# Four weight buffers at the start of the u stage, expert rows of v gathered from the end of the u stage with a pause, and the second gate tile loaded earlier

## The chip, the cores and the metric

The kernel runs on one core of one Trainium2 chip as a single launch. The metric is device time in microseconds (us), the median of several runs. Before the change it is 2059.68 us, the median of 3 runs that lie between 2057.51 and 2063.43. The profiled execution, from which every duration below is taken, took 2052.94 us, and its instructions span 2051.2 us.

## The reference, cut to what matters

The reference is a decoder trunk of two layers on 256 tokens of width 1024. Each layer adds three things to x: a mixer (stick-breaking attention beside chunkwise retention), cross-attention to 256 memory rows, and an expert network with product-key retrieval. A final RMSNorm ends it. The change touches the expert network alone:

```python
def peer_ffn(h, w_pq, sub_keys, expert_u, expert_v):     # shortened
    q = (h @ w_pq).reshape(B, S, PEER_HEADS, 2, PEER_DQ // 2)
    scores = jnp.einsum('bshpd,hpkd->bshpk', q, sub_keys)
    top_s, top_i = lax.top_k(scores, K)                  # 16 of 128 keys, twice per head
    ...                                                  # 16 best of the 256 sums: expert_idx, gate
    u = jnp.take(expert_u, ic, axis=0)
    a = jnp.einsum('cd,chkd->chk', hc, u)
    w = gc * jax.nn.gelu(a, approximate=False)
    return jnp.einsum('chk,chkd->cd', w, jnp.take(expert_v, ic, axis=0))
```

There are 16384 experts of one neuron each, and a token uses 8 heads x 16 of them. `peer_u` and `peer_v` are 64 MB per layer each.

## The kernel before, in words

For 224 of the 256 tokens the kernel does not gather experts. It multiplies the whole of `peer_u` with the tokens (the **u stage**), applies the GELU to all 16384 x 224 products, multiplies them by gates that are zero for every expert a token did not choose, and multiplies the result with the whole of `peer_v` (the **v stage**). For the last 32 tokens it gathers rows of `peer_u` and `peer_v` (4 per step and token, on 128 partitions), 32 steps each.

**The weight stream.** All weights pass through the class `Stream`. A *pair* is 1 MB (128 partitions x 2048 floats) and serves two *units* of 128 x 1024. A layer has 42 pairs ahead of the experts, then 64 pairs for u and 64 for v, so the u stage has units 0 to 127, and so has the v stage. `load` issues the pair loads on SP's queue, into one of two own buffers `raw`, or into a buffer of the list `more` while the pair's number is not over `last`. `prep` splits a unit for the fp32r matmuls: ScalarE copies it to `hi` (L74), VectorE subtracts to get `lo` (L76). It stands two units ahead of the matmuls; there are three `hi` and `lo` tiles. After the second half of a pair is split its buffer is free, and `load` issues the next pair into it; SP's queue waits for that subtraction. A unit of u is 24 matmuls of 224 columns (L1150, L1151, L1153), a unit of v 16 (8 of 448 columns, 8 of 224; L1213, L1215).

**Side work.** The code is a fixed order on each engine. After each unit `side.tick()` advances every side task by one step (`yield`), so a side task's instructions stand between those of the units:

- `peer_task` selects the experts, scatters the gates of tokens 128 to 223 into the DRAM table `gd` by indirect adds on GpSimd (L920), and builds the gates of tokens 0 to 127 in the SBUF tile `gt` (16 x 1024 floats per partition, `g_build`).
- `gather_u` gathers rows of u (L1028 on GpSimd) into two buffers `rows` and reduces them on VectorE (L1069) to the weights `wg`. It ends when all 32 are reduced and all scatters are issued.
- `gather_v` gathers 32 times rows of v (L1028) into the same two buffers, and VectorE adds each, weighted, to `hacc` (L1091, L1093). Before the change it is started when the v stage starts, and does one gather every 3, 3 and 4 units. At its end it adds the sums to x in four additions (L1102 to L1110).

**The activated values.** In the u stage `ev_u` writes the GELU of tokens 128 to 223 into `act`, a tile of 128 x 128 x 96 floats, two of the 128 slices after every second unit, in order. The other 128 tokens go to DRAM (`tdr`), or straight into `gt` once that is complete.

**The gate tiles.** `w_load(n)` loads for pair n of v the gates from `gd` (L1174) and the activated values from `tdr` (L1179); its tiles are `tt_` for even n and `oh` for odd n, two buffers of each name. `w_mul` multiplies them on GpSimd and VectorE (L1185, L1187), `w_hi` and `w_lo` split the product (ScalarE L1202, VectorE L1207). The v matmuls of units 2n and 2n+1 wait for `w_lo(n)`. `w_load(0)` waits for the last scatters.

In the v stage two parts of `gt` that have been used join the list `more` after units 18 and 34, so that from there the stream has three and then four buffers; in the u stage it has two.

Of the kernel before, what the change touches and what calls it, by code (L numbers as in the profile page):

```python
# [132 lines left out]
def build(tc, ctx, a):  # L133
# [27 lines left out]
    st = Stream(tc, ctx, units)  # L161
    side = Side()
# [34 lines left out]
    def unit(f):  # L197
        hi, lo = st.get()
        f(hi, lo)
        flush()  # L200
        side.tick()
# [55 lines left out]
    def b_units(src, n, evac, first=0):  # L257

        for i in range(first, first + n):
            if i % 2 == 0:  # L260
                ps = mm.tile([128, 2, 256], F32, name="mm")

            def f(hi, lo):
                h3 = hi.rearrange("p (k n) -> p k n", k=KT)
                l3 = lo.rearrange("p (k n) -> p k n", k=KT)
                o = ps[:, i % 2]
                for k in range(KT):
                    T.matmul(o, h3[:, k], src[:, k, 0:256], start=(k == 0), stop=False)  # L268
                    T.matmul(o, h3[:, k], src[:, k, 256:512], start=False, stop=False)  # L269
                for k in range(KT):  # L270
                    T.matmul(o, l3[:, k], src[:, k, 0:256], start=False, stop=(k == KT - 1))  # L271
            unit(f)
            if i % 2:
                pend.append(lambda i=i, ps=ps: evac(i // 2, ps))
# [92 lines left out]
    for l in range(L):  # L367
# [654 lines left out]
        def rows_():  # L1022
            return gp.tile([128, D], F32, name="rows", bufs=2)

        def gather(rows, j):

            r = rows_()
            G.indirect_dma_start(r, None, rows, bass.IndirectOffsetOnAxis(ap=eg[:, 0, j:j + 1], axis=0))  # L1028
            return r
        go = []  # L1030

        def gather_u():

            hr = gp.tile([128, D], F32, name="hacc")
            gn = rows_()
            row = a["peer_norm"][l]
            nc.scalar.dma_start(gn, bass.AP(tensor=row.tensor, offset=row.offset, ap=[[0, 128], [1, D]]))
            V.tensor_scalar(hr[T0:128], x[T0:128, 1], rx[T0:128, 1:2], None, op0=OP.mult)
            yield
            yield  # L1040
            for q in range(3):
                nc.sync.dma_start(hr[TG * q:TG * q + TG], hr[T0:128])
            yield
            yield
            V.tensor_mul(hr, hr, gn)
            pool_us, since, n, done, ready = 0.0, 0, 0, 0, 0
            rs = deque()
            while done < 32 or held:
                if go and not ready:
                    ready = 1  # L1050
                    for q in range(4):
                        nc.sync.dma_start(eg[TG * q:TG * q + TG], ge[T0:128, :, 32 * q:32 * q + 32])
                pool_us = min(pool_us + POOL[0], 2 * POOL[0])
                while pool_us > 0:
                    if ready > 2 and n < 32 and len(rs) < 2 and (since >= 2 or not held):
                        rs.append((gather(u_rows, n), ready))
                        n, since = n + 1, 0
                        pool_us -= POOL[2]
                    elif held:
                        if next(held[0], held) is held:  # L1060
                            held.popleft()
                            continue
                        since += 1
                        pool_us -= POOL[1]
                    else:
                        break
                if rs and rs[0][1] + 3 < ready:
                    r, _ = rs.popleft()
                    V.tensor_tensor_reduce(r, r, hr, 1.0, 0.0, op0=OP.mult, op1=OP.add,  # L1069
                                           accum_out=wg[:, done:done + 1])  # L1070
                    credit[0] -= 1.25
                    done += 1
                ready += ready > 0
                yield
            A.activation(wg, wg, AF.Gelu)
            yield
            V.tensor_mul(wg, wg, eg.bitcast(F32)[:, 1])

        def gather_v():

            for _ in range(2):
                yield
            acc = gp.tile([128, D], F32, name="hacc")
            rs = deque()
            for j in range(33):
                if j < 32:
                    rs.append(gather(v_rows, j))
                if j >= 1:
                    r = rs.popleft()
                    if j == 1:  # L1090
                        V.tensor_scalar(acc, r, wg[:, 0:1], None, op0=OP.mult)  # L1091
                    else:
                        V.scalar_tensor_tensor(acc, r, wg[:, j - 1:j], acc, op0=OP.mult, op1=OP.add)  # L1093
                for _ in range(3 + (j % 3 == 2)):
                    yield
            parts = []
            for q in range(3):
                r = rows_()
                nc.sync.dma_start(r[T0:128], acc[TG * q:TG * q + TG])
                parts.append(r)  # L1100
                if q == 1:
                    V.tensor_add(x[T0:128, 1], x[T0:128, 1], acc[T0:128])  # L1102
                    yield
                    yield
                    yield
                    V.tensor_add(x[T0:128, 1], x[T0:128, 1], parts.pop(0)[T0:128])
            for r in parts:
                yield
                yield
                V.tensor_add(x[T0:128, 1], x[T0:128, 1], r[T0:128])  # L1110
# [15 lines left out]
        credit = [0.0]  # L1126
        t_p = side.add(paced(peer_task(), credit, RATE))
        t_g = side.add(gather_u())
        b_units(hTp, 14, ev_q, 2)
        flush()  # L1130
        side.drain(t_h)
# [2 lines left out]
        act = pool(c_g0, "act", side="right").tile([128, 128, T0], F32, name="act")  # L1134
# [3 lines left out]
        def u_units(first, n):  # L1138

            for i in range(first, first + n):  # L1140
                if i % 2 == 0:
                    u_ps[0] = mm.tile([128, 2, 256], F32, name="mm")
                ps = u_ps[0]

                def f(hi, lo):
                    h3 = hi.rearrange("p (k n) -> p k n", k=KT)
                    l3 = lo.rearrange("p (k n) -> p k n", k=KT)
                    o = ps[:, i % 2, 0:TD]
                    for k in range(KT):
                        T.matmul(o, h3[:, k], hT[:, k, 0:TD], start=(k == 0), stop=False)  # L1150
                        T.matmul(o, h3[:, k], hT[:, k, 256:256 + TD], start=False, stop=False)  # L1151
                    for k in range(KT):
                        T.matmul(o, l3[:, k], hT[:, k, 0:TD], start=False, stop=(k == KT - 1))  # L1153
                unit(f)
                if i % 2:
                    pend.append(lambda i=i, ps=ps: ev_u(i // 2, ps))
# [53 lines left out]
        def v_mm(i, w, hi, lo, ds=(4, 5, 6, 7, 0, 1, 2, 3)):  # L1210

            for d in ds:
                T.matmul(out[d][:, 0:2 * TD], hi[:, d * 128:d * 128 + 128], w[:, i % 2].rearrange("p a t -> p (a t)"),  # L1213
                         start=(i == 0), stop=False, skip_group_check=True)
                T.matmul(out[d][:, 0:TD], lo[:, d * 128:d * 128 + 128], w[:, i % 2, 0],  # L1215
                         start=False, stop=(i == 127), skip_group_check=True)
        u_units(0, 124)
        flush()
        assert not t_p in side.tasks and not t_g in side.tasks
        w_load(0)  # L1220
        u_units(124, 2)
        w_mul(0)
        w_hi(0)
# [1 line left out]
        w_lo(0)  # L1225
        u_units(127, 1)
        flush()
        w_load(1)
        w_load(2)
        c_ps.close()  # L1230
        ops = pool(c_ps, "ops", space=PS)
        out = [mm.tile([128, 512], F32, name="mm") for d in range(4)]
        out += [ops.tile([128, 512], F32, name=f"out{d}") for d in range(4, 8)]
        t_v = side.add(gather_v())
        st.last = (st.n + 126) // 2
        for i in range(126):
            n = i // 2
            if i % 2 == 0:
                for m in {0: (), 1: (3, 4), 2: (5, 6)}.get(n, (n + 4,)):
                    w_load(m)  # L1240
                if n in (9, 17):
                    st.more.append(gt[0][:, 2 * n - 18:2 * n - 2].rearrange("p c t -> p (c t)"))
                w_mul(n + 1)
                w = ww.pop(n)
            else:
                w_lo(n + 1)

            def f(hi, lo):
                v_mm(i, w, hi, lo)
                if i % 2 == 0:  # L1250
                    w_hi(n + 1)
            unit(f)
# [151 lines left out]
```

## Time and profile before

| | before |
|---|---|
| median of 3 runs | 2059.68 us (2057.51 to 2063.43) |
| the profiled execution's own time | 2052.94 us |
| span of its instructions | 2051.2 us |
| TensorE busy (matmuls) | 2000.3 us, 98% of the span |
| VectorE / ScalarE / GpSimd busy | 1590.0 / 1109.5 / 787.5 us |
| mean granted TensorE clock | 0.994 of full speed |
| DMA | 499.63 MB, 244 GB/s on average |
| u stages, first to last unit | 304 to 692 us and 1317 to 1707 us |
| v stages, first to last unit | 692 to 1020 us and 1707 to 2038 us |

The u stage starts with the first matmul of L1150 and the v stage with the first of L1213. TensorE's busy time is the union of its matmuls; a gap in it is time in which it waited. "Idle before" and "<-" name what ended such a wait.

### The profile page before, as it was taken

To read this page: it belongs to the slowest core of one execution; us is meant where nothing else is said; L and a number is where in the kernel's file an instruction comes from. 1 tells how busy PE (TensorE), PEld (TensorE's weight loads), DVE (VectorE), ACT (ScalarE), POOL (GpSimd) and SP (SyncE) were. 2 spreads that over 40 slices of the span, in tenths; PEclk is the share of its full clock that TensorE was granted. 3 is DMA by queue.
4 is the path that set the end of the run, shared out by engine and by line. 5 is a ranking of instruction groups with operands and counts; after the bars stand their busy time and mean duration, and the time that the engine had idled before them with its cause. 6 is when DMAs were issued, how large, how long until landed. Compare 5 with 4: busy or idle time off the path is not lost.

```text
span 2051.2 us, 37324 instructions
## 1 busy us (share of the span) xinstructions
PE 2000.3 (98%) x14564; PEld 1906.1 (93%) x14564; DVE 1590.0 (78%) x2691; ACT 1109.5 (54%) x1573; POOL 787.5 (38%) x569
## 2 busy tenths in 40 slices
PE   8999999999999999999999999999999998999997
PEld 7899899999999989999988998999999998999997
DVE  5775598988877578888876756899888765888887
ACT  5645555544566545555566445654456664455554
POOL 0120028778765123332112100477767632232321
PEclk9999999999999999999999999999999999999999
DMA  7655457899876689999566545578988766999983
GB/s 251 222 208 179 149 178 197 244 284 285 266 230 199 239 312 340 322 318 314 171 229 249 182 165 178 162 211 262 281 263 281 228 182 231 327 339 323 320 298 127
DMA packets 189250, 499.63 MB, mean 244 GB/s; under 512 B 77329, under 2 KB 124561, under 8 KB 144401
## 3 DMA queue, kind: packets, MB, share of 16 engines
q1 hardware_dynamic: 138800, 421.12, 59.5%
q0 software_dynamic: 47104, 67.23, 13.0%
q10 hardware_dynamic: 3168, 8.90, 1.3%
q8 instruction: 113, 1.85, 0.4%
q14 instruction: 65, 0.52, 0.1%
HBM read 478.40 MB, written 33.91 MB: 250 GB/s over the span
## 4 chain that ended last, share of the span: by engine, by line
PE 70%; DVE 12%; DMA 10%; issue 5%; ACT 3%; SPq 0%; POOL 0%; ACTq 0%; POOLq 0%; DVEq 0%
PE mm L1213 8%; PE out L1213 8%; DVE lo L76 6%; PE mm L1151 5%; PE mm L1150 5%; PE mm L1153 5%; DMA raw<-u 5%; PE mm L1215 4%; PE out L1215 4%; PE mm L211 4%; PE mm L213 4%; PE mm L212 4%; PE mm L269 3%; PE mm L271 3%; PE mm L268 3%
## 5 line engine op out<-in xcount | busy, mean ns | idle before, releaser
L74 ACT CAST hi<-raw 128x1024 fp32r<-128x1024 f32 x580 | 607.6, 1052 | 573.0 <-DMA raw<-u 196.1
L76 DVE TENSOR_TENSOR lo<-raw,hi 128x1024 fp32r<-128x1024 f32 x580 | 714.1, 1238 | 259.8 <-ACT hi L74 252.8
L920 POOL DMA_INDIRECT gd<-gv,gi x256 | 438.8, 1714 | 187.6 <-issue 82.8
L1150 PE MATMUL mm<-hT,hi 128*128 128x224 f32 x2048 | 480.9, 279 | 8.9 <-ACT hi L74 8.5
L1151 PE MATMUL mm<-hT,hi 128*128 128x224 f32 x2048 | 474.2, 276 | 0.0
L1150 PEld LDWEIGHTS mm<-hT,hi 128*128 128x128 f32 x2048 | 396.8, 194 | 11.4 <-ACT hi L74 10.3
L1151 PEld LDWEIGHTS mm<-hT,hi 128*128 128x128 f32 x2048 | 396.2, 193 | 0.0
L1213 PE MATMUL out<-hT,hi 128*128 128x448 f32 x1008 | 333.5, 376 | 12.7 <-DVE hT L1207 12.7
L1213 PE MATMUL mm<-hT,hi 128*128 128x448 f32 x1008 | 331.1, 374 | 0.0
L1153 PE MATMUL mm<-hT,lo 128*128 128x224 f32 x2048 | 274.2, 277 | 3.5 <-DVE lo L76 3.5
L1215 PE MATMUL out<-hT,lo 128*128 128x224 f32 x1008 | 266.8, 265 | 0.0
L1215 PE MATMUL mm<-hT,lo 128*128 128x224 f32 x1008 | 266.4, 264 | 0.0
L1153 PEld LDWEIGHTS mm<-hT,lo 128*128 128x128 f32 x2048 | 251.4, 193 | 5.5 <-DVE lo L76 4.8
L1213 PEld LDWEIGHTS out<-hT,hi 128*128 128x128 f32 x1008 | 189.6, 188 | 30.5 <-DVE hT L1207 16.2
L1213 PEld LDWEIGHTS mm<-hT,hi 128*128 128x128 f32 x1008 | 189.3, 188 | 14.4
L1215 PEld LDWEIGHTS out<-hT,lo 128*128 128x128 f32 x1008 | 192.8, 191 | 0.0
L1215 PEld LDWEIGHTS mm<-hT,lo 128*128 128x128 f32 x1008 | 192.5, 191 | 0.0
L1028 POOL DMA_INDIRECT rows<-v_rows,eg x64 | 87.0, 1359 | 217.9 <-DVE hacc L1093 205.6
L74 ACT CAST hi<-gt 128x1024 fp32r<-128x1024 f32 x100 | 104.9, 1049 | 116.0 <-PE mm L1213 93.3
L76 DVE TENSOR_TENSOR lo<-gt,hi 128x1024 fp32r<-128x1024 f32 x100 | 126.0, 1260 | 37.4 <-ACT hi L74 37.1
L277 POOL TENSOR_TENSOR rstd<-rstd,mhalf 128x2 f32<-128x2 f32 (+1 forms) x8 | 5.5, 688 | 302.7 <-DVE rstd L317 302.7
L1028 POOL DMA_INDIRECT rows<-u_rows,eg x64 | 97.9, 1530 | 57.4 <-DVE wg L1069 39.8
(710 smaller groups left out, 3274.9 us busy)
## 6 DMA issues: line engine op xcount, KB each, us to landing
raw<-u SPq DMA_DIRECT2D x128, 1024.0 KB
raw<-v SPq DMA_DIRECT2D x78, 1024.0 KB
gt<-v SPq DMA_DIRECT2D x50, 1024.0 KB
raw<-w_in_a SPq DMA_DIRECT2D x20, 1024.0 KB
gd<-zeros SPq DMA_DIRECT2D x64, 256.0 KB
raw<-pq SPq DMA_DIRECT2D x16, 1024.0 KB
raw<-wkv_b SPq DMA_DIRECT2D x8, 1024.0 KB
raw<-w_out SPq DMA_DIRECT2D x8, 1024.0 KB
```

What stands on the lines that cost most here:

```text
L74: self.nc.scalar.copy(hi, r)
L76: self.nc.vector.tensor_sub(lo, r, hi.bitcast(F32))
L211: T.matmul(ps[tt], sh, h3[:, kk], start=(k == 0), stop=False)
L212: T.matmul(ps[tt], sl, h3[:, kk], start=False, stop=False)
L213: T.matmul(ps[tt], sh, l3[:, kk], start=False, stop=(k == KT - 1))
L920: i_ = G.indirect_dma_start(gd[l], bass.IndirectOffsetOnAxis(ap=gi[0:T0, h, c:c + 1], axis=0), gv[0:T0, h, c:c + 1], None, compute_op=OP.a ...
L1028: G.indirect_dma_start(r, None, rows, bass.IndirectOffsetOnAxis(ap=eg[:, 0, j:j + 1], axis=0))
L1150: T.matmul(o, h3[:, k], hT[:, k, 0:TD], start=(k == 0), stop=False)
L1151: T.matmul(o, h3[:, k], hT[:, k, 256:256 + TD], start=False, stop=False)
L1153: T.matmul(o, l3[:, k], hT[:, k, 0:TD], start=False, stop=(k == KT - 1))
L1213: T.matmul(out[d][:, 0:2 * TD], hi[:, d * 128:d * 128 + 128], w[:, i % 2].rearrange("p a t -> p (a t)"), start=(i == 0), stop=False, skip_ ...
L1215: T.matmul(out[d][:, 0:TD], lo[:, d * 128:d * 128 + 128], w[:, i % 2, 0], start=False, stop=(i == 127), skip_group_check=True)
```

## The change

Three edits. First, when the u stage starts, the last third of `act` (two parts of 2048 floats per partition, slices 85 and up) joins the list `more`, and `last` allows it for the first 40 of the 64 pairs, units 0 to 79. `act` slice 84 and up are written after unit 85. The list is cleared when the v stage starts. Second, `gather_v` is added as a side task together with `gather_u` and begins when `gather_u` has ended. Its spacing follows the number of units since the start of the u stage: 2 units before unit 122, then until unit 146 (unit 18 of v) a pause, then (246 - unit) / (rounds left). Third, `w_load(1)` stands right behind `w_load(0)`, four units earlier than before.

```diff
-        go = []
+        go, u0 = [], []
 ...
         def gather_v():
 
-            for _ in range(2):
+            while t_g in side.tasks:
                 yield
 ...
-                for _ in range(3 + (j % 3 == 2)):
+                at = st.n - u0[0]
+                for _ in range(2 if at < 122 else 146 - at if at < 146 else max((246 - at) // (33 - j), 1)):
                     yield
 ...
         t_g = side.add(gather_u())
+        t_v = side.add(gather_v())
 ...
+        u0.append(st.n)
+        st.last = (st.n + 78) // 2
+        for i in (4, 5):
+            st.more.append(act.rearrange("p i t -> p (i t)")[:, 2048 * i:2048 * i + 2048])
         u_units(0, 124)
         flush()
         assert not t_p in side.tasks and not t_g in side.tasks
         w_load(0)
+        w_load(1)
         u_units(124, 2)
 ...
         flush()
-        w_load(1)
         w_load(2)
 ...
-        t_v = side.add(gather_v())
         st.last = (st.n + 126) // 2
+        st.more.clear()
```

The line numbers behind the second edit grow by 1 or 2: L1163 (the store to `tdr`) is L1165 after, L1174 and L1179 are L1176 and L1181, L1185 is L1187.

SP's queue at the start of the first u stage. `raw0` and `raw1` are the stream's own buffers, `act` is the tile of activated values, `tdr` stores are those of `ev_u`. Before:

```order
L62 DMA raw0_71<-u 128x2048
L62 DMA raw1_72<-u 128x2048
L62 DMA raw0_71<-u 128x2048
L62 DMA raw1_72<-u 128x2048
L1163 DMA tdr_99<-tt__3155 128x256
L62 DMA raw0_71<-u 128x2048
L1163 DMA tdr_99<-tt__3248 128x256
```

Now:

```order
L62 DMA raw0_71<-u 128x2048
L62 DMA raw1_72<-u 128x2048
L62 DMA raw0_71<-u 128x2048
L62 DMA act_3045<-u 128x2048 x2
L62 DMA raw1_72<-u 128x2048
L1165 DMA tdr_99<-tt__3157 128x256
L62 DMA raw0_71<-u 128x2048
L1165 DMA tdr_99<-tt__3250 128x256
L62 DMA act_3045<-u 128x2048
```

Two more pairs are issued ahead of the first store, so that each later load stands four pairs ahead of its use and not two.

SP's queue where the u stage ends; `tt_` and `oh` are gate tiles, `gd0` is the gate table. Before:

```order
L1163 DMA tdr_99<-tt__8048 128x256
L62 DMA raw0_71<-v 128x2048
L1174 DMA tt__8084<-gd0_97 128x2x96
L1179 DMA tt__8084<-tdr_99 128x2x128
L62 DMA raw1_72<-v 128x2048
L62 DMA raw0_71<-v 128x2048
L1174 DMA oh_8216<-gd0_97 128x2x96
L1179 DMA oh_8216<-tdr_99 128x2x128
L1174 DMA tt__8219<-gd0_97 128x2x96
```

Now:

```order
L1165 DMA tdr_99<-tt__8054 128x256
L62 DMA raw1_72<-v 128x2048
L1176 DMA tt__8090<-gd0_97 128x2x96
L1181 DMA tt__8090<-tdr_99 128x2x128
L1176 DMA oh_8093<-gd0_97 128x2x96
L1181 DMA oh_8093<-tdr_99 128x2x128
L62 DMA raw0_71<-v 128x2048
L62 DMA raw1_72<-v 128x2048
L1176 DMA tt__8225<-gd0_97 128x2x96
```

The second gate tile (`oh_8216` before, `oh_8093` now) moved ahead of two pair loads of v.

GpSimd at the same place; `rows<-v_rows` are the gathers, the L1185 (now L1187) rows are `w_mul`. Before:

```order
L920 DMA gd0_97<-gv_4027,gi_4028 2097152x1 x14
L1185 TENSOR_TENSOR tt__8084<-tt__8084,act_3045 128x2x96
L1185 TENSOR_TENSOR oh_8216<-oh_8216,act_3045 128x2x96
L1185 TENSOR_TENSOR tt__8219<-tt__8219,act_3045 128x2x96
L1028 DMA rows_8310<-v_rows,eg_2351 128x1024
L1185 TENSOR_TENSOR oh_8280<-oh_8280,act_3045 128x2x96
L1028 DMA rows_8385<-v_rows,eg_2351 128x1024
L1185 TENSOR_TENSOR tt__8283<-tt__8283,act_3045 128x2x96
L1185 TENSOR_TENSOR oh_8334<-oh_8334,act_3045 128x2x96
L1028 DMA rows_8462<-v_rows,eg_2351 128x1024
```

Now:

```order
L920 DMA gd0_97<-gv_4029,gi_4030 2097152x1 x14
L1028 DMA rows_7936<-v_rows,eg_2351 128x1024
L1028 DMA rows_8020<-v_rows,eg_2351 128x1024
L1187 TENSOR_TENSOR tt__8090<-tt__8090,act_3045 128x2x96
L1187 TENSOR_TENSOR oh_8093<-oh_8093,act_3045 128x2x96
L1187 TENSOR_TENSOR tt__8225<-tt__8225,act_3045 128x2x96
L1187 TENSOR_TENSOR oh_8286<-oh_8286,act_3045 128x2x96
L1187 TENSOR_TENSOR tt__8289<-tt__8289,act_3045 128x2x96
L1187 TENSOR_TENSOR oh_8337<-oh_8337,act_3045 128x2x96
```

Two gathers stand ahead of the first gate product; the third follows the tenth product (`oh_8484`), where before five gathers stand in between.

## Rows read from the trace of the kernel before

**Rows 1.** The page: span, TensorE, and who TensorE waited for (waits view).

```profile
span 2051.2 us, 37324 instructions
...
PE 2000.3 (98%) x14564; PEld 1906.1 (93%) x14564; DVE 1590.0 (78%) x2691; ACT 1109.5 (54%) x1573; POOL 787.5 (38%) x569
...
PE out L1213 <- DVE hT L1207: 12.7, 12, 3.0
PE mm L1150 <- ACT hi L74: 8.5, 6, 2.6
...
PE mm L1153 <- DVE lo L76: 3.5, 7, 0.9
...
PE sps L986 <- DVE gs L981: 1.7, 2, 1.3
```

**Rows 2.** Windows: stretch, length, busy us of five engines (instructions), clock, DMA share, GB/s.

```profile
300.00:400.00 100.00, 99.86 (x892) 99.68 (x891) 92.82 (x299) 59.18 (x92) 79.37 (x46) 1.00 0.76 214
400.00:550.00 150.00, 143.26 (x1236) 140.73 (x1236) 129.93 (x272) 74.11 (x114) 115.37 (x71) 0.99 0.91 280
675.00:775.00 100.00, 94.11 (x634) 88.90 (x633) 70.43 (x79) 47.33 (x62) 24.28 (x28) 1.00 0.82 287
775.00:800.00 25.00, 25.00 (x162) 23.86 (x160) 21.69 (x24) 12.98 (x16) 7.96 (x8) 1.00 0.98 357
825.00:975.00 150.00, 150.00 (x960) 143.18 (x959) 128.31 (x139) 78.11 (x90) 48.09 (x47) 1.00 0.93 317
1300.00:1400.00 100.00, 99.87 (x886) 99.68 (x885) 92.77 (x289) 60.88 (x96) 72.31 (x42) 1.00 0.70 199
1400.00:1575.00 175.00, 167.87 (x1438) 165.87 (x1437) 150.37 (x326) 85.58 (x131) 129.66 (x81) 0.97 0.89 275
1700.00:1775.00 75.00, 68.16 (x436) 63.82 (x435) 50.90 (x59) 33.02 (x43) 19.06 (x21) 0.98 0.81 277
```

**Rows 3.** Timeline of u: SP's issues, ScalarE's splits, TensorE: start, length, what, [idle before].

```profile
328.88 0.33 SPq L62 DMA_DIRECT2D raw<-u  x1
...
334.14 1.05 ACT L74 CAST hi<-raw 128x1024 fp32r<-128x1024 f32 x1 [2.82 <-DMA raw<-u]
...
463.68 0.33 SPq L62 DMA_DIRECT2D raw<-u  x1
...
471.04 1.04 ACT L74 CAST hi<-raw 128x1024 fp32r<-128x1024 f32 x1 [5.02 <-DVE wg L1069]
...
472.14 0.37 PE L1150 MATMUL mm<-hT,hi 128*128 128x224 f32 x1 [1.70 <-ACT hi L74]
```

**Rows 4.** Timeline where the v stage begins: first and second gate tile, then one pair load.

```profile
681.23 0.61 SPq L1179 DMA_DIRECT2D tt__8084<-tdr  x1
...
691.61 0.39 SPq L1174 DMA_DIRECT2D oh<-gd  x1
...
696.59 0.60 POOL L1185 TENSOR_TENSOR oh<-oh,act 128x192 f32<-128x192 f32 x1 [10.58 <-DMA oh<-gd]
...
698.93 0.61 DVE L1207 TENSOR_TENSOR hT<-oh,hT 128x448 fp32r<-128x448 f32 x1
...
699.60 0.47 PE L1213 MATMUL out<-hT,hi 128*128 128x448 f32 x1 [2.56 <-DVE hT L1207]
...
712.19 0.97 POOL L1028 DMA_INDIRECT rows<-v_rows,eg  x1 [0.15 <-DMA tt__8337<-gd]
...
715.56 0.35 SPq L62 DMA_DIRECT2D raw<-v  x1
...
722.73 1.05 ACT L74 CAST hi<-raw 128x1024 fp32r<-128x1024 f32 x1 [3.23 <-DMA raw<-v]
```

**Rows 5.** Timeline of GpSimd: the last scatter of layer 0 and what follows it.

```profile
646.54 1.46 POOL L920 DMA_INDIRECT gd<-gv,gi  x1 [0.30 <-issue]
685.40 0.60 POOL L1185 TENSOR_TENSOR tt__8084<-tt__8084,act 128x192 f32<-128x192 f32 x1 [37.40 <-DMA tt__8084<-gd]
```

**Rows 6.** VectorE by lines: count, busy us, mean ns, idle before and what ended it.

```profile
L1093 DVE SCALAR_TENSOR_TENSOR hacc<-rows,wg,hacc 128x1024 f32<-128x1024 f32 x62 | 81.7, 1317 | 0.0
L1069 DVE CUSTOM_DVE_ANT_0 rows<-rows,hacc 128x1024 f32<-128x1024 f32 x64 | 77.7, 1214 | 1.5 <-DMA rows<-u_rows,eg 1.5
```

## The prediction

> **What bounds the kernel now.** I read the page first: TensorE's matmuls fill 2000.3 us of a span of 2051.2 [rows 1], so work taken off another engine gains nothing, and only TensorE's gaps can be won. Then the windows, to see where the gaps lie. In the first 100 us of each u stage TensorE is busy for 99.86 and 99.87 us, and from 775 us on in v it is never idle: 150.00 of 150 [rows 2]. A unit costs 100 us x 24 / 892 = 2.69 us in u and 150 x 16 / 960 = 2.50 us in v. Between these stretches lie four with losses, and the change aims at all four:
>
> - u, layer 0, 400 to 550: 150 - 143.26 = 6.7 us idle, and a mean granted clock of 0.99 [rows 2]. The clock has two levels, 1.2 and 2.4 GHz, and time at the lower one is half lost, so 0.99 costs 150 x 0.01 = 1.5 us. Sum 8.2.
> - u, layer 1, 1400 to 1575: 7.1 idle, 0.97 x 175 costs 5.3. Sum 12.4.
> - v, layer 0, 675 to 775: 5.9 idle, clock 1.00. Sum 5.9. The u stage's last units fill TensorE up to 692, so this is v's.
> - v, layer 1, 1700 to 1775: 6.8 idle, 0.98 x 75 costs 1.5. Sum 8.3.
>
> That is 20.6 us in u and 14.2 in v, 34.8 together. The rest of the span's idle time is in stages that the change leaves alone.
>
> Then the waits, to see what ended those gaps: in v the split gates `hT` of VectorE (12.7 us, 12 times), in u `hi` (8.5), `lo` (3.5) and the expert slots `gs` (1.7) [rows 1]. These engines only pass it on, and the timeline shows who is late. At 328.88 a pair load of u is issued and used at 334.14, 5.3 us later, with TensorE whole. At 463.68 one is issued and used at 471.04, 7.4 us later. ScalarE's gap of 5.02 us there is put down to a VectorE instruction, but the `hi` copy reads nothing but the pair, so I take it as the load. TensorE then idles 1.70 us [rows 3]. The u stage has two buffers, so a load has little more than one pair's time, 2 x 2.69 = 5.4 us, and 7.4 is too much. DMA share explains it: 0.76 of the time in 300 to 400, 0.91 in 400 to 550, where gathers and scatters run beside the loads [rows 2].
>
> At the start of v two things are late. The load of the second gate tile is issued at 691.61, because it stands behind two pair loads in SP's queue, and its product on GpSimd starts at 696.59. The split ends at 699.54, and TensorE has waited 2.56 us [rows 4]. Later the pair loads of v are late, again with two buffers: issued 715.56, used 722.73, 7.2 us against the 5.0 that a pair's units take, with a gather of v rows begun at 712.19 beside it [rows 4].
>
> **The change, part by part.**
>
> *Four buffers for u pairs 0 to 39.* No instruction is added, each load is issued two pairs sooner, and SP waits for the same subtractions as before. The cushion is 4 units x 2.69 = 10.8 us of TensorE's work, filled in 300 to 400, where the share is 0.76 and 0.70 [rows 2]. Even if the loads came no faster afterwards, 10.8 us would cover the 8.2 of layer 0 and all but 1.6 of the 12.4 of layer 1. Would they come as fast? The same transfers in less time make the share 0.91 x 150 / 141.8 = 0.96 and 0.89 x 175 / 162.6 = 0.96, and 0.98 is held at 775 to 800 with TensorE whole [rows 2]. Two things remain. The 1.7 us for `gs` are VectorE's, no load's. And VectorE, busy 129.93 us of 150, would have to do that in 141.8: 0.92, where 0.93 is borne in 300 to 400 without loss [rows 2]; still, its splits stand behind selection work, so I leave 1 us per layer. Gain 20.6 - 1.7 - 2 = 16.9. Bounds: 0 if VectorE takes the loads' place at once, 20.6 if all goes.
>
> The Trainium skill's page "DMA: Bandwidth & Descriptors" (Specifications) puts the limit of one core's HBM traffic near 358 GB/s. The trace agrees that no more is reached (357 at 775 to 800), but by that rule the 280 GB/s of the u stretch would leave a fifth free, and the busy share leaves a tenth. By the rule the loads catch up at once and the sum is the 34.8 of the second rival below. I go by the share.
>
> *Second gates sooner.* One `w_load` moves past two pair loads on SP, two DMAs in all. It needs tile `oh`, long free, and the scatters that `w_load(0)` has waited for. Issued right behind that one, whose last transfer goes out at 681.23 [rows 4], it comes some 9 us earlier and has landed before the v stage. That takes 2.56 us in layer 0. In layer 1 the longest wait for `hT` is 3.0 [rows 1], and the 1.5 us of clock lies in the same stretch. Gain 7.1, between 0 (the third tile, issued at the same point as before, is late instead) and 7.1. I take 7.1, as the third is needed two units later.
>
> *v rows with a pause.* Before, 5 of the 32 gathers fall into units 0 to 17 of v. Now the first two stand right behind the last scatter, where GpSimd sits idle for 37.4 us [rows 5], and none in units 0 to 17. What is left of v's loss, 14.2 - 7.1 = 7.1 us, I put down to pair loads slowed by gathers. Without them a load should take nearer to the 5.3 us of the calm u stretch than to 7.2. I keep 1 us per layer and take 5.1, between 0 and 7.1.
>
> *What it costs.* The other 30 gathers come every 3 units from unit 17 on, not every 3 1/3, while the third and fourth buffers of v are still filling. Their share of the DMA time rises by a tenth; the total stood at 0.93 to 0.98 there without loss [rows 2]. I take 1 us per layer, bounds 0 and 5 (2% of the 250 us, if the DMA were full). The four additions to x move 5 units towards v's end, each of them little beside VectorE's 128.31 busy of 150 [rows 2]: nothing. In the u stage the two early accumulations fall to its last units, where VectorE has room: nothing.
>
> Sum: 16.9 + 7.1 + 5.1 - 2 = 27.1 us. The profiled execution, 2052.94 us for its span of 2051.2, would come to 2025.8. The median of the runs before, 2059.68, stands 6.7 above it; I predict for the median: 2059.68 - 27.1 = 2032.6, say 2032.
>
> **Rivals.**
>
> *All of it goes.* If only the latency of loads was short and VectorE keeps up, all 34.8 are won: 2025. For it: TensorE whole at a share of 0.98. Against it: the `gs` wait, which no load causes.
>
> *VectorE takes the loads' place in u.* Its splits and the selection work run in one queue, and it was 0.87 busy in the lossy stretch with TensorE waiting. If half of u's 20.6 comes back as waits for `lo` and `gs`, the time is 2059.7 - 10.3 - 10.2 = 2039. For it: the waits for `lo` and `gs` exist now, 5.2 us [rows 1]. Against it: 0.93 without loss at 300 to 400.
>
> *Not what it says.* If the last subtractions that free the buffers, and not the loads, are what is late, more buffers are just as late, and only the second gates count: 2052.
>
> *Slower.* Four outstanding pair loads delay the gathers of u rows, and VectorE, which takes its work in order, waits for each at L1069 with the splits behind it. Now that costs 1.5 us in 64 reductions [rows 6]. From 27.1 / 64 = 0.42 us for each it eats the gain; at 0.6 us it gives 2071. Against it: in v the same gathers run beside four buffers, and L1093 never waited for a row, 0.0 us in 62 [rows 6].
>
> The Trainium skill's page "DMA: Bandwidth & Descriptors" (Queues, rings and completion order) says that each DMA engine takes turns between the queues it has work for. By that rule the gathers, which go by another queue than SP's, are not starved by a longer SP queue; the zero at L1093 agrees.
>
> **How the numbers follow.** Chances: forecast 0.55 (2026 to 2038), all of it 0.15 (2025, down to 2019 with the gaps too short for these windows), VectorE 0.18 (2036 to 2049), not what it says 0.07, slower 0.05. The range from 2019 to 2049 holds the first three, 0.88. About 0.3%, 6 us, can be told from no change. The first three are faster by more than that, and half of the fourth: 0.91. Within it: 0.04. Slower: 0.05.
>
> **What would show it.** In the profile after, TensorE is busy for at least 148 us of the 150 from 400 to 550 and the clock is 1.00 there; ScalarE's waits for u loads fall below half; the wait for `hT` falls from 12.7 to under 4 us; and the second gate product on GpSimd stands before the first v matmul. If TensorE's gaps in u stay and are ended by `lo` with no load behind them, the second rival holds. If they stay with loads behind them, my reading of the cushion is wrong. New gaps 45 to 100 us into v would show the tighter gathers too cheap.

## The result and the profile after

The changed kernel takes 2033.74 us (median of 4 runs, 2029.67 to 2034.00), the kernel before in the same comparison 2058.60 us (4 runs). The ratio is 0.9894, with an interval from 0.9873 to 0.9916: faster by 24.9 us. 2032 was predicted. By the ratio the gain is 21.8 us. The profiled execution took 2034.0 us, 18.9 less than the profiled one of before, which was itself 5.7 us under the median of its four runs.

The page, the waits of TensorE and the windows of the changed kernel, with the stretches and columns of [rows 1, 2]:

```profile
span 2032.2 us, 37325 instructions
...
PE 1990.7 (98%) x14564; PEld 1900.9 (94%) x14564; DVE 1583.5 (78%) x2691; ACT 1118.5 (55%) x1573; POOL 797.8 (39%) x569
...
PE mm L1155 <- DVE lo L76: 14.7, 10, 4.5
...
PE sps L986 <- DVE gs L981: 2.6, 2, 1.3
```

```profile
300.00:400.00 100.00, 99.71 (x892) 99.52 (x890) 92.75 (x297) 61.03 (x93) 79.01 (x46) 1.00 0.80 239
400.00:550.00 150.00, 141.97 (x1234) 140.41 (x1233) 128.51 (x274) 74.56 (x110) 117.88 (x71) 0.98 0.85 264
675.00:775.00 100.00, 100.00 (x682) 96.18 (x681) 73.76 (x84) 52.88 (x66) 22.65 (x25) 1.00 0.85 291
825.00:975.00 150.00, 150.00 (x959) 143.19 (x958) 127.28 (x138) 78.09 (x91) 51.92 (x47) 1.00 0.94 319
1400.00:1575.00 175.00, 165.69 (x1448) 163.88 (x1447) 148.83 (x309) 89.20 (x130) 133.75 (x80) 0.99 0.86 265
1700.00:1775.00 75.00, 75.00 (x481) 71.58 (x480) 57.96 (x66) 38.68 (x45) 19.15 (x22) 1.00 0.90 308
```

Two things are to be seen. The start of v is whole in both layers (100.00 of 100, 75.00 of 75), and `hT` is gone from the waits. But u has lost as much as before: 8.0 us idle in 400 to 550 where [rows 2] had 6.7, 9.3 in 1400 to 1575 where they had 7.1. The clock is 0.98 where it was 0.99 in the one and 0.99 where it was 0.97 in the other, so idle time and clock together come to 22 us, where the prediction read 20.6. Only the name of the wait changed, from `hi` to `lo`.

The start of v in layer 0, as in [rows 4, 5] (timeline: start, length, queue or engine, line, what, idle before):

```profile
647.38 1.73 POOL L1028 DMA_INDIRECT rows<-v_rows,eg  x1 [0.30 <-DVE oh L1006]
649.41 0.96 POOL L1028 DMA_INDIRECT rows<-v_rows,eg  x1 [0.30 <-issue]
...
680.96 0.59 SPq L1176 DMA_DIRECT2D oh<-gd  x1
...
685.38 0.61 POOL L1187 TENSOR_TENSOR oh<-oh,act 128x192 f32<-128x192 f32 x1
...
690.94 0.37 PE L1215 MATMUL out<-oh,hi 128*128 128x448 f32 x1
```

The second gate tile is loaded at 680.96, not 691.61, and its product ends before the first v matmul. The first v rows are gathered while GpSimd has nothing else.

Now u. First who waits for whom. ScalarE's wait for pair loads of u, before and then after (total, times, longest):

```profile
ACT hi L74 <- DMA raw<-u: 196.1, 72, 6.8
```

```profile
ACT hi L74 <- DMA raw<-u: 33.3, 18, 3.6
```

The loads are no longer late. VectorE's line that answers to [rows 6] says what is:

```profile
L1069 DVE CUSTOM_DVE_ANT_0 rows<-rows,hacc 128x1024 f32<-128x1024 f32 x64 | 77.8, 1216 | 35.3 <-DMA rows<-u_rows,eg 29.6 <-issue 5.7
```

The reductions of gathered u rows waited 1.5 us before and wait 35.3 now. The worst of them, in the timeline of the changed kernel, GpSimd first, then VectorE, ScalarE and TensorE:

```profile
403.45 1.46 POOL L920 DMA_INDIRECT gd<-gv,gi  x1 [0.30 <-issue]
410.04 2.37 POOL L920 DMA_INDIRECT gd<-gv,gi  x1 [5.14 <-issue]
412.72 1.54 POOL L1028 DMA_INDIRECT rows<-u_rows,eg  x1 [0.31 <-issue]
...
422.33 1.23 DVE L1069 CUSTOM_DVE_ANT_0 rows<-rows,hacc 128x1024 f32<-128x1024 f32 x1 [7.35 <-DMA rows<-u_rows,eg]
423.48 0.08 DVE L1069 DVE_READ_ACCUMULATOR2_ANT wg<- 128x1 f32 x1
423.48 2.36 DVE L76 TENSOR_TENSOR lo<-raw,hi 128x1024 fp32r<-128x1024 f32 x2
...
424.79 1.04 ACT L74 CAST hi<-raw 128x1024 fp32r<-128x1024 f32 x1 [5.66 <-DVE lo L76]
...
424.76 2.05 PE L1155 MATMUL mm<-hT,lo 128*128 128x224 f32 x8 [4.53 <-DVE lo L76]
```

GpSimd works through its list of scatters and gathers, issues the gather only at 412.72, VectorE stands at the reduction for 7.35 us with the next two splits behind it in its queue, and TensorE idles 4.53 us. From the gather's end (414.26) to the reduction it is 8.1 us, where a row takes some 5 to land on average (below), so about 3 of the 7.35 us are a slow transfer and not a late issue. After its idle time TensorE takes 2.05 us for eight matmuls that took 1.06 before: the granted clock from 424.76 to 426.80 is 0.50, the lower level.

### The profile page after: what moved, and what is told of

It is laid out like the page before. It is cut to its first block, busy times and chain, and to the rows that moved or that the text cites. A ratio compares the mean times of both kernels' runs of the same rounds, so it can differ in the third digit from the quotient of the medians.

```text
span 2032.2 us, 37325 instructions
## 1 busy us (share of the span) xinstructions
PE 1990.7 (98%) x14564; PEld 1900.9 (94%) x14564; DVE 1583.5 (78%) x2691; ACT 1118.5 (55%) x1573; POOL 797.8 (39%) x569
## 5 line engine op out<-in xcount | busy, mean ns | idle before, releaser
L76 DVE TENSOR_TENSOR lo<-raw,hi 128x1024 fp32r<-128x1024 f32 x504 | 620.3, 1239 | 222.9 <-ACT hi L74 221.3
L74 ACT CAST hi<-raw 128x1024 fp32r<-128x1024 f32 x504 | 528.0, 1052 | 440.5 <-PE mm L1215 129.9
L920 POOL DMA_INDIRECT gd<-gv,gi x256 | 444.4, 1736 | 186.8 <-issue 84.6
L1028 POOL DMA_INDIRECT rows<-v_rows,eg x64 | 102.5, 1602 | 228.2 <-DVE hacc L1093 214.7
L74 ACT CAST hi<-act 128x1024 fp32r<-128x1024 f32 x76 | 79.4, 1050 | 76.2 <-PE mm L1153 59.1
```

What stands on the lines that cost most here:

```text
L74: self.nc.scalar.copy(hi, r)
L76: self.nc.vector.tensor_sub(lo, r, hi.bitcast(F32))
L920: i_ = G.indirect_dma_start(gd[l], bass.IndirectOffsetOnAxis(ap=gi[0:T0, h, c:c + 1], axis=0), gv[0:T0, h, c:c + 1], None, compute_op=OP.a ...
```

## The experiments

Three theories stood at the start. **1:** GpSimd's list holds more than it can do there, so the rows come late, and the splits behind them. **2:** four outstanding loads slow the gathers' transfers. **3:** VectorE's own splits and selection work are the bound. The kernel before was run beside each group of experiments; its median moved between 2051.84 and 2059.56 us from group to group, so across groups the ratios say more than the times. Below, the length of a stage is from its first matmul to the first of the next stage for u, and from its first unit to its last for v, both layers, from the profiled execution.

**The three edits, one at a time on the kernel before.** The four u buffers alone:

```diff
+        st.last = (st.n + 78) // 2
+        for i in (4, 5):
+            st.more.append(act.rearrange("p i t -> p (i t)")[:, 2048 * i:2048 * i + 2048])
         u_units(0, 124)
 ...
+        st.more.clear()
```

> The kernel before with the four u buffers alone (loads two pairs sooner, for pairs 0 to 39); second gates and v rows stay as before. Theory 1, gathered rows: GpSimd, full with scatters and gathers from 400 to 490 us, sets when the u rows come, VectorE waits for them in order at L1069 with the splits behind, and the loads' share of the loss only changes its name. It expects the u stages no shorter than 2 us under before's 387.4 and 389.6 us, L1069 waiting 25 to 40 us instead of 1.5, and the total 0 to 3 us under before. Theory 2, transfers: four outstanding loads delay the gathers' own transfers. The same waits, but the mean time from a gather's end on GpSimd to its landing rises from before's 4.8 and 5.0 us to over 6. The recorded prediction's term: 16.9 us faster.

Measured: 2051.35 us against 2059.56, ratio 0.9965 (0.9947 to 0.9983), so 7.2 us faster by the ratio. L1069 waits 31.4 us for rows, as theory 1 has it; the total is more than it allowed and far less than the prediction's term. The u stages are 388.4 and 385.3 us, the second 4.3 under before's, also more than theory 1 allowed. From the end of a gather on GpSimd to the last of its 128 packets it takes 4.89 and 5.22 us on average (4.79 and 5.01 before, 5.07 and 4.73 in the changed kernel), not over 6: theory 2 falls. The Trainium skill's page "DMA: Bandwidth & Descriptors" (Queues, rings and completion order) says that each DMA engine takes turns between its queues; these times agree.

The second gate tile's load alone:

```diff
         w_load(0)
+        w_load(1)
 ...
-        w_load(1)
         w_load(2)
```

> The kernel before with the second gate tile's load moved ahead of the last pair loads of u, nothing else. The recorded prediction's term is 7.1 us (2.56 in layer 0, 3.0 and 1.5 of clock in layer 1): v stages 323.4 and 323.8 us instead of 326.0 and 328.3, no wait of TensorE for hT over 1 us. Rival: the loads of the pairs behind are late by as much, and the total is 0 to 3 us under before.

Measured: 2047.17 us, ratio 0.9944 (0.9919 to 0.9969), 11.5 us by the ratio. The v stages are 322.8 and 322.7 us instead of 326.0 and 328.3: 3.2 + 5.6 = 8.8. Waits for `hT` remain, 5.8 us, the longest 1.7, where none over 1 was expected.

The v rows from the end of u with the pause, alone (the second edit of the diff above):

```diff
-            for _ in range(2):
+            while t_g in side.tasks:
 ...
-                for _ in range(3 + (j % 3 == 2)):
+                at = st.n - u0[0]
+                for _ in range(2 if at < 122 else 146 - at if at < 146 else max((246 - at) // (33 - j), 1)):
 ...
```

> The kernel before with the v rows gathered from the u stage's end and the pause, nothing else; the second gate tile's load stays late. The recorded prediction's term is 5.1 us, less 2 for tighter gathers later: 3 in all. If the tighter gathers cost nothing, as the changed kernel's v units of 2.50 us from unit 18 on say, and the two edits add up to the 17.3 us by which its v stages are shorter, this one gives 7 to 11 us, with the wait for hT at the v stage's third unit left (2 to 3 us per layer).

Measured: 2049.46 us, ratio 0.9960 (0.9941 to 0.9979), 8.2 us by the ratio. The v stages are 323.2 and 323.0 us: 2.8 + 5.3 = 8.1, with two waits for `hT` left:

```profile
PE out L1215 <- DVE hT L1209: 5.5, 2, 2.8
```

So the two edits at v give 8.8 and 8.1, together 16.9; in the changed kernel both v stages are 318.5 us, 17.3 less than before. They add up, and no loss to the tighter gathers is seen.

**The changed kernel without the four u buffers:**

```diff
-        st.last = (st.n + 78) // 2
-        for i in (4, 5):
-            st.more.append(act.rearrange("p i t -> p (i t)")[:, 2048 * i:2048 * i + 2048])
 ...
-        st.more.clear()
```

> The changed kernel without the four u buffers (two, as in the kernel before); second gates and v rows as changed. If the four buffers only change the name of u's waits, as the two profiles say (u 387.4 and 389.6 us before, 387.8 and 388.5 after), the time is within 3 us of the changed kernel's and the other two edits carry all of the gain: ratio to before 0.988 to 0.992. If they bring what the four buffers brought alone in timed runs, 8.2 us under the kernel before (interval 3.5 to 10.9), it is 4 to 11 us slower than the changed kernel: ratio 0.991 to 0.996. The recorded prediction's term: 16.9 slower.

Measured: 2040.30 us, ratio 0.9942 (0.9920 to 0.9964): 6.6 us over the changed kernel's median, 7.2 over its one run beside this group (the next paragraph) and 10 by the ratios. The buffers alone gave 7.2. Here ScalarE waits 214.0 us for u loads again and L1069 2.5 us for rows.

**The changed kernel profiled once more:**

> The changed kernel once more, for a second profile of the u stages. If one profile is enough to tell, 387.8 and 388.5 us return within 1.5 us; the two profiles with late u rows so far (the changed kernel's and the one with four buffers alone, 385.7 and 382.6) let me expect 382 to 389, with waits at L1069 of 25 us or more.

2033.07 us, with u stages of 388.2 and 384.3 us, and 31.7 us of waits for rows at L1069. These two profiles differ by 4 us in a u stage, and over kernels with the same u code the spread is larger: with two buffers layer 0 takes 386.8 to 395.1 us. Over the four kernels with two buffers at the old pace (before, second gate, v rows, without buffers) the u stages average 390.1 and 389.5 us, over the three with four buffers 388.1 and 386.0. By these averages the buffers give 2.0 + 3.5 = 5.5 us. That is rough (without the one of 395.1 us layer 0 gives 0.3), but it agrees with the 7 us or so of the timed runs, and 16.9 were predicted.

**Deeper gathers.** Four row buffers instead of two, reductions eight units behind the gather, and three pair buffers:

```diff
 ...
-                    if ready > 2 and n < 32 and len(rs) < 2 and (since >= 2 or not held):
-                        rs.append((gather(u_rows, n), ready))
+                    deep = bool(xr) and st.n - u0[0] < 72
+                    if ready > 2 and n < 32 and len(rs) < (4 if deep else 2) and (since >= 2 or not held):
+                        e_ = xr[n % 4 - 2] if deep and n % 4 > 1 else None
+                        rs.append((gather(u_rows, n, e_), ready))
 ...
-                if rs and rs[0][1] + 3 < ready:
+                if rs and rs[0][1] + (7 if xr and st.n - u0[0] < 76 else 3) < ready:
 ...
```

> The changed kernel with the u rows gathered earlier: while the unit is below 72, gathers use four row buffers instead of two (two of them in free memory of the activated values), each reduction is put eight units behind its gather instead of four until unit 76, and the stream has three pair buffers instead of four in the u stage, to pair 49 instead of 39. Theory 1 (gathered rows late by GpSimd's pace, VectorE waits for them in order): waits at L1069 fall from 29.6 to under 8 us, waits of TensorE for lo in u from 14.7 to under 5, each u stage is 5 to 10 us shorter than the changed kernel's 387.8 and 388.5, and the time is 12 to 18 us under the changed kernel's. Theory 2 (four outstanding loads slow the gathers): about half of that, since three are still outstanding. Theory 3 (VectorE's own splits and selection are the bound): the waits at L1069 go and TensorE's for lo and gs stay; at most 4 us.

Measured: 2039.25 us, ratio 0.9896 (0.9872 to 0.9919): no better than the changed kernel. All three expectations missed. The windows show why:

```profile
400.00:500.00 100.00, 100.00 (x897) 100.00 (x897) 92.02 (x227) 53.67 (x81) 74.41 (x45) 1.00 0.96 298
500.00:550.00 50.00, 39.38 (x317) 38.69 (x316) 34.28 (x43) 19.83 (x30) 37.68 (x24) 0.90 0.75 220
1400.00:1480.00 80.00, 80.00 (x719) 80.00 (x718) 74.20 (x197) 39.11 (x60) 56.29 (x33) 1.00 0.95 303
1480.00:1560.00 80.00, 67.93 (x567) 67.25 (x567) 59.72 (x97) 38.53 (x55) 62.35 (x41) 0.91 0.80 245
```

TensorE is whole for 100 us with VectorE 0.92 busy, the very share at which the prediction wanted it, and with three loads and up to four gathers outstanding at a DMA share of 0.96. That is against theories 2 and 3. As soon as the deeper buffers end, everything is paid back: 10.6 us idle in 50. GpSimd's lines from 400 to 500 us in this run (busy us, mean ns, idle just before; `act` holds the two added row buffers) show that it fell behind meanwhile:

```profile
L920 POOL DMA_INDIRECT gd<-gv,gi x30 | 55.9, 1865 | 21.3 <-issue 12.9 <-DMA gd<-gv,gi 8.4
L1028 POOL DMA_INDIRECT act<-u_rows,eg x8 | 11.4, 1419 | 2.4 <-issue 0.9 <-ACT hi L74 0.3 <-DVE g L964 0.3
L1028 POOL DMA_INDIRECT rows<-u_rows,eg x7 | 9.3, 1325 | 2.1 <-issue 1.8 <-DVE tv L816 0.3
```

`gather_u` hands GpSimd its work by a budget, the constant `POOL` of the code: every unit adds 2.75 us, a scatter takes 2.25 of it and a gather 1.6. In these 100 us TensorE does 100 / 2.69 = 37.2 units, but GpSimd's 30 scatters and 15 gathers are 30 x 2.25 + 15 x 1.6 = 91.5 us of the budget, 33.3 units. It falls some 4 units back with nothing but its own work to wait for. So the buffers held its lag for a while and did not take it away. The run does not tell this lag apart from the step back from four row buffers to two: between 512 and 533 us GpSimd issues scatters and no gather, which adds to the loss there.

In the changed kernel itself, GpSimd's lines from 400 to 500 us:

```profile
L920 POOL DMA_INDIRECT gd<-gv,gi x32 | 58.6, 1831 | 18.9 <-issue 14.3 <-DMA gd<-gv,gi 4.6
L1028 POOL DMA_INDIRECT rows<-u_rows,eg x14 | 19.7, 1409 | 5.3 <-issue 1.8 <-DVE wg L1069 1.6 <-DVE bp L821 0.9
```

Busy and idle together are 77.5 us for 32 scatters and 25.0 for 14 gathers: 102.5 us. That the sum is about the length of the stretch says nothing by itself; what counts is that the idle part is hardly free time. Some 0.30 us lie before nearly every instruction, and the code makes the first of a head's 16 scatters wait for the earlier head's (5.14 us at 410.04, 4.59 at 461.70); one wait of 1.33 us is for VectorE. By the budget this work is 32 x 2.25 + 14 x 1.6 = 94.4 us, 34.3 units, which a whole TensorE does in 34.3 x 2.69 = 92.3 us. GpSimd takes 102.5. By this estimate it could keep up at an allowance of 94.4 x 2.69 / 102.5 = 2.48.

**Another pace for the scatters** tests that. Nothing but the budget's allowance for a unit changes:

```diff
-                pool_us = min(pool_us + POOL[0], 2 * POOL[0])
+                pool_us = min(pool_us + (2.75 if not u0 else 2.35 if st.n - u0[0] < 80 else 3.3), 2 * POOL[0])
```

> The changed kernel with GpSimd's scatters of u put out at another pace: the planner's allowance is 2.35 us a unit until unit 80 and 3.3 from there, instead of 2.75 throughout; gathers, buffers and everything else stay. Theory 1 (GpSimd's program holds more than it can do between 400 and 500 us, so the u rows come late and VectorE waits for them at L1069 with splits behind): the 29.6 us of waits at L1069 fall below 12, TensorE's waits for lo in u from 14.7 below 7, each u stage is 4 to 9 us shorter and the time 8 to 16 us under the changed kernel's; scatters end later in u, which may add a wait of TensorE at v's start. Theory 3 (VectorE's own work is the bound): u as it is, 0 to 3 us.

Measured: 2017.41 us (6 runs) against 2051.84 for the kernel before in that comparison, ratio 0.9831 (0.9803 to 0.9858), an interval that ends below that of the changed kernel. The waits and windows of this kernel:

```profile
PE mm L1155 <- DVE lo L76: 1.9, 3, 0.7
...
DVE rows L1069 <- DMA rows<-u_rows,eg: 11.9, 5, 4.0
```

```profile
400.00:550.00 150.00, 149.52 (x1337) 149.15 (x1336) 137.49 (x283) 82.65 (x121) 110.53 (x67) 1.00 0.87 275
1400.00:1575.00 175.00, 172.95 (x1535) 171.70 (x1534) 151.94 (x295) 96.70 (x139) 128.20 (x78) 1.00 0.86 269
```

The u stages are 375.7 and 379.5 us, 12.1 and 9.0 under the changed kernel's profile, and the time is 16.3 us under its median and 13 by the ratios: as theory 1 has it, at the upper end of its ranges or past it. In the first of these stretches VectorE does more per microsecond than in the changed kernel (137.49 us of work against 128.51) and TensorE hardly waits for it.

**Half of the scatters.** Every second scatter is left out, which leaves out half of the gates of tokens 128 to 223 (the expectation's "tokens 0 to 127" is a slip):

```diff
+                    if c % 2:
+                        G.nop()
+                        if c == TOPK - 1:
+                            late[:] = now
+                        yield
+                        continue
```

> The changed kernel with every second scatter of the gate sums left out (it leaves out half of the gates of tokens 0 to 127 of the second tile's scattered part), all else in the same order. Theory 1: GpSimd is free in time, no wait at L1069 over 1 us, no wait of TensorE for lo in u over 1 us; what is left in u are the 2.6 us for gs; each u stage 6 to 9 us shorter than 387.8 and 388.5. Theory 3 (VectorE's own splits and selection are the bound): TensorE's waits for lo stay at 10 us or more.

One run of 2012.06 us, with u stages of 376.8 and 376.1 us:

```profile
PE mm L1161 <- DVE lo L76: 1.4, 3, 0.7
...
DVE rows L1075 <- DMA rows<-u_rows,eg: 3.9, 2, 3.1
```

Theory 3 falls. The gain is larger than the 6 to 9 us a stage that theory 1 gave, and one wait for rows of 3.1 us is left where none over 1 was expected. With half of GpSimd's scatters gone u is no shorter than with the paced ones: by this one run the pace takes all that there was. A rival is that with fewer scatters in the way the rows' transfers land sooner, and GpSimd's time does not matter. It does not hold: from a gather's end to its last packet it takes 5.48 and 5.55 us here and 4.87 and 4.96 with the paced scatters, on average no sooner than in the changed kernel (5.07 and 4.73).

**The pace with two buffers.** The last two edits, the pace without the four buffers:

> The changed kernel with the slower pace of the scatters (2.35 us a unit until unit 80, then 3.3) and with two u buffers instead of four. Theory 1 in full (loads and gathered rows are two limits side by side, and the later one counts): with two buffers the loads stay late, so the pace brings little by itself; u stages 380 to 388 us, TensorE's waits in u ended by hi with loads behind them, 0 to 6 us under the same kernel at the old pace (median 2040). Rival: the rows alone were the limit of u, and the four buffers are not needed at this pace; u stages 373 to 378 us and the time within 3 us of the 2017 that buffers and pace gave together.

Measured: 2040.55 us, ratio 0.9925 (0.9898 to 0.9952); u stages 389.2 and 391.8, a little over the 380 to 388 expected. The wait is again that of before, and no reduction waits for a row (TensorE's wait for `gs` is longer, 6.4 us):

```profile
PE mm L1152 <- ACT hi L74: 7.1, 10, 2.3
...
ACT hi L74 <- DMA raw<-u: 186.2, 70, 5.5
```

So the pace without the buffers gives nothing that can be told (2040.30 us without it; by the ratios, 0.9942 and 0.9925, 3.5 us with intervals that overlap, and the u stages are no shorter), the buffers without the pace give some 7, and both give 22.9. Two limits stand side by side, and the late loads hid the late rows.

**Two more paces** (2.55, then 3.3; and 2.2, then 4.0), with four buffers:

> The changed kernel with a pace between: allowance 2.55 us a unit until unit 80, 3.3 from there (2.75 throughout in the changed kernel, 2.35 and 3.3 in the run that gave 2017 us). If GpSimd's lag behind the planned order is what the u rows wait for, the result lies between: waits at L1069 of 13 to 28 us, u stages 376 to 383 us, time 2018 to 2029 us.

> The changed kernel with a slower pace still: 2.2 us a unit until unit 80, 4.0 from there. If the pace only had to be what GpSimd can do, L1069's waits fall under 6 us and the u stages are those of the kernel with half of the scatters, 373 to 374 us: time 2012 to 2018. Against it: more scatters are left for the last 40 units of u, the last of them end later, and the gate tiles that are loaded behind them come late at v's start: 1 to 5 us back per layer.

At 2.55 it is 2017.77 us (0.9816, 0.9790 to 0.9842), u 377.2 and 381.0: as good as 2.35, and just under the 2018 to 2029 expected; L1069's 12.2 us of waits for rows are under their 13 as well. It is above the 2.48 worked out, so that estimate is good to a few per cent at best. At 2.2 and 4.0 it is 2027.28 us (0.9873, 0.9848 to 0.9899), u 382.7 and 383.9, worse, and outside the 2012 to 2018 of the expectation, but not by the late gate tiles that I had named: the loss is in u. The scatters put off come back at 4.0 us a unit, where units 80 to 120 take 3.45 us each: by the estimate above, 94.4 / 4.0 x 3.45 = 81 us for what takes 102.5. (At 3.3 it gives 99 us, short as well, and no such wait is seen there: the estimate shows the direction and not the size.) The rows are late there:

```profile
DVE rows L1069 <- DMA rows<-u_rows,eg: 36.2, 11, 5.3
```

Of these, 15.8 us in 4 waits lie between 600 and 645 us, in units 103 to 115 of layer 0. The fastest version is the changed kernel with 2.35 and 3.3 (or 2.55): 2017 us, 16.3 below the change by the medians and 13 by the ratios.

## Why the prediction was right in the sum and wrong in its parts

**The losses.** 20.6 us in u and 14.2 in v were read rightly as places, and a little low. All of v's came back, 17.3 us; from unit 34 on a unit of v takes 2.51 us in both kernels, so all of it lies at the start of v, where the prediction's sum of idle time and clock has 3.1 us less. With the scatters paced u's came back as well: 14.4 and 10.0 us under the averages with two buffers.

**Four buffers in u: 16.9 predicted, 5.5 measured by the profiles and some 7 by timed runs.** This step failed. The prediction's cushion covered the loads, and it did so (196.1 to 33.3 us). What it put next in line was VectorE's busy time, "0.92, where 0.93 is borne", and that was borne here too. What it did not work out is GpSimd: 115.37 us busy of 150 [rows 2] looked free, but busy time leaves out the 0.30 us between instructions and the waits between heads; with them the list takes 102.5 us where a whole TensorE gives it 92.3. Before, late loads stretched the units, so GpSimd could nearly keep up, and L1069 waited 1.5 us. The runs that pace the scatters or leave out half of them show that this is the cause: with the same four buffers most of u's loss is then gone (0.5 and 2.1 us idle in the two stretches).

**The rivals.** "All of it goes" (the 34.8 that the prediction once calls its second rival) did not come with the change itself, and 2017 us with the paced scatters is below its 2025. "Not what it says" falls with the load waits. "VectorE takes the loads' place" gave the outcome of u, and more than half came back (20.6 less 5.5), but its cause was wrong: VectorE was not short of time, it stood in order behind late rows. That wait is the one of "Slower", but not for the reason given there, loads that delay the gathers: on average the rows landed as fast as before. The reductions waited 35.3 / 64 = 0.55 us each, beyond the 0.42 from which it was to eat the gain, and yet the kernel is faster: these waits came in the loads' place, not on top, and the v term stood apart. The argument against "Slower", no wait at L1093 in v, says nothing of u, since in v GpSimd has no scatters to do.

**Second gates: 7.1 predicted, 8.8 measured. v rows: 5.1 less 2 predicted, 8.1 measured.** The mechanisms were right. The sum was 7.1 us low: 2 us of load waits that I kept and of which TensorE has none left, 2 charged for tighter gathers (the stretch 825 to 975 has 150.00 of 150 at a share of 0.94, and the v units there stay at 2.51 us), and the 3.1 by which the loss itself was larger.

**The sum.** 5.5 + 17.3 = 22.8 by the averages of the profiles, 24.9 by the medians, 27.1 predicted. The total was right by luck: 11.4 us too much in u stood against 7.1 too little in v.

Of the signs named beforehand, three came: loads below half, `hT` under 4 us, the second product ahead of the first v matmul. TensorE's 148 of 150 did not (141.97 at 0.98), and the gaps ended by `lo` without a load behind them were the sign that the prediction gave for "VectorE takes the loads' place". That sign fits any late VectorE and could not tell a busy one from one that waits.

## What to carry to other kernels

Before a wait is priced as gained, list every other thing that the waiting engine's queue needs in that stretch and work out whether each supplier can keep up with the faster pace: issue gaps and dependences count as its time, not the busy share alone. A deeper buffer does not help against a supplier that is slower on average: here it kept TensorE whole for 100 us and the loss came behind. Two limits of similar size hide each other, and removing one shows little until the other goes as well.

## What the hardware showed that was not expected

An indirect add of 96 values of 4 bytes holds GpSimd longer than a gather of 128 rows of 4 KB: 1736 ns against 1510 for rows of u and 1602 for rows of v, on average over the changed kernel, besides some 0.30 us before each. So here it is the number of such instructions, not their bytes, that fills GpSimd. And u units at a DMA share of 0.96 lose nothing: 100.00 us of 100 in the run with deeper gathers.
